# A decoder layer's token mixer issued in the order of a written table, with the compressed branch made for four heads at once

## The chip, the cores and the metric

The kernel runs on one core of a Trainium2 chip. Its time is the time of one execution on the device in microseconds, the median of several runs. In the rows, PE is TensorE (the matrix engine), DVE is VectorE, ACT is ScalarE, POOL is GpSimd and SP is SyncE, which here only issues transfers.

## The reference

One layer on x of 512 rows by 1024 columns in float32: a normed token mixer and a normed SwiGLU, both with a residual.

```python
h = rms_norm(x, attn_pre_norm)
mix = hybrid_mixer(h, ...) # one input projection, two kinds of heads, one output projection
x = x + rms_norm(mix, attn_post_norm)
h = rms_norm(x, ffn_pre_norm)
f = (silu(h @ w_gate) * (h @ w_up)) @ w_down
x = x + rms_norm(f, ffn_post_norm)
```

The mixer has four differential heads (two causal softmax maps of 512 by 512 each, the second subtracted with a factor, times values of 128 columns, then a norm of the head) and eight sparse heads in two groups of four. A sparse head sums three branches, each weighted by a sigmoid gate: selected blocks (with this length all blocks are chosen), a window, and a compressed branch. The compressed branch has 31 compressed keys and values for the whole group, made from blocks of 32 rows by a small two-layer network:

```python
sc = einsum('bghqd,bgnd->bghqn', qb, kc) * scale
pc = masked_softmax(sc, cmp_end[None, :] <= qpos[:, None])
o_cmp = einsum('bghqn,bgnd->bghqd', pc, vc)
...
return gb[..., 0:1] * o_cmp + gb[..., 1:2] * o_slc + gb[..., 2:3] * o_win
```

## The kernel before, in words

Rows are handled in four tiles of 128 (index i). Every factor of a large product is split into a high and a low part in a reduced float32 (names ending in h and l, or whi and wlo for weights, ws for output weights), and a product is three products: high times high, low times high, high times low. A weight is loaded as wraw by SP, ScalarE makes whi and VectorE the difference wlo; wraw, whi and wlo have three buffers each, so a load waits until the load three before it has been split.

The opening loads x as columns (xraw), scales it (xh by ScalarE at L213, xl by VectorE at L222), squares and adds it, and TensorE sums the squares over the columns (ssum), from which VectorE makes the rows' factors rstd; rb is rstd spread over all partitions by TensorE, and the rotary tables are multiplied with it. The products with the input weights (fm, and dv for values) don't wait for rstd; what is made of them does.

A softmax map: scores (sc) by TensorE, the masked scores and the maximum in one instruction by VectorE (L510, tile p, maximum nm), the exponential by ScalarE with the sum in l, the division of rows by l (POOL and ScalarE in sparse heads, POOL and VectorE in differential ones), transposes by TensorE (tr), a high copy by ScalarE (pth, L525) and a low one by VectorE (ptl, L526), and the product with the values (av, avn). A sparse head's result lies in half of opair, and each second head is split into oh and ol. A differential head ends with a norm (ms, rr, rs, rsb, sq) ahead of its oh and ol.

In the compressed branch each sparse head has a score bank scc of which it uses 128 columns (four row tiles times 32), nmc (maximum), pc, l, and pcs: the high and low parts, each twice, so that four 128-column transposes (trc, pct) give a left factor of 128 partitions for the product with vcs, whose four blocks of partitions hold the compressed values high and low.

The products with the output weights are made in two parts: mixp (four of the eight blocks of heads, D0, D1 and the first two sparse pairs) are made during the later heads and copied to SBUF (rope), mix (the other four) for the first two row tiles are made at the end. The norm behind (first instruction mixt) adds both. F0 and F1 are the splits of the first two blocks of feed-forward weights; gain and x are the loads that the norm reads (u is mixt times gain). Behind them come the feed-forward products gu, gw and acc.

Step functions are called in the order of a string:

```python
ORDER = (
    "C v1 q1 q0 k1 cv n1 W0 k0 n0 ck s v0 g W4 D0 D1 W1 N0 N1 N2 N3 W5 N4 W2 W3 N5 D2 M0 N6 W6 W7 M1 M2 M3 D3 F0 F1 N7"
)
...
    def nsa_head(*a):
        with tc.high_priority(offset=HP):
            nsa_head_(*a)
```

Each step writes all its instructions at once; a list scheduler with estimated times then chooses for each engine which ready instruction comes next, with the heads preferred. So the string sets priorities, and not the order on an engine. Tile pools add waits: PSUM has two banks of mm (projections and mix), three of sc, two of tr and one of av, and there are 36 slots of 128 by 512 for split data.

## Time and profile before

| | |
|---|---|
| median of three runs | 669.98 us (669.73 to 670.91) |
| profiled execution | 670.32 us, its span 668.5 us |
| granted TensorE clock, mean | 0.986 |
| TensorE busy | 640.7 us, 96% |
| VectorE busy | 559.3 us, 84% |
| ScalarE busy | 388.6 us, 58% |
| GpSimd busy | 76.4 us, 11% |

A row of a group reads: line, engine, operation, out<-in by the program's names, partitions by elements, xcount, then busy us, mean ns of one, and the idle time of its engine ahead with what ended it. A row of the timeline starts with its start in us and its length. A row of waits gives engine, tile and line, what it waited for, the total in us, how often, and the longest. A row of the stretches gives from:to, length, busy us of each engine (with the number of instructions), the granted TensorE clock, the share of the transfer engines and GB/s.

### The profile page before, as it was taken

The page shows a single profiled execution, that of the slowest core. Times are in us where ns is not written, and L with a number is a line of the kernel's source. Part 1 is how long each engine was busy: PE and PEld are TensorE (multiplying, and loading weights), DVE is VectorE, ACT ScalarE, POOL GpSimd, SP SyncE. Part 2 cuts the span into 40 slices and gives each one's busy share as a digit, 9 for nine tenths or more (in the row PEclk, how much of TensorE's full clock was granted, in tenths as well). Part 3 has the DMA queues.
Part 4 walks back from the last instruction along what each step waited for, and adds up shares of the span by engine and source line. Part 5 has one row for each costly group of instructions (what it writes and reads, how often), then busy time and mean ns, then how long its engine had stood idle before and what let it go on. Part 6 is the DMA issues. An engine that isn't in the chain of part 4 may idle for free.

```text
span 668.5 us, 11185 instructions
## 1 busy us (share of the span) xinstructions
PE 640.7 (96%) x4099; PEld 573.1 (86%) x4099; DVE 559.3 (84%) x1114; ACT 388.6 (58%) x820; POOL 76.4 (11%) x86
## 2 busy tenths in 40 slices
PE   8999999999899998888899999999999999999995
PEld 5988788899778787777898999999999998888884
DVE  4878797897999987768999998888888639999966
ACT  6443453657799766635646555555555547665424
POOL 0000000020755532501100000000000000000023
PEclk9999999999999999979989999999999999999998
DMA  8445767771030530136213323323223217562443
GB/s 307 163 142 204 270 223 280 273 284 56 17 127 18 173 104 24 64 106 241 96 64 126 126 97 114 108 96 122 99 95 127 96 49 251 189 219 96 172 112 126
DMA packets 29735, 94.50 MB, mean 141 GB/s; under 512 B 3824, under 2 KB 4720, under 8 KB 28784
## 3 DMA queue, kind: packets, MB, share of 16 engines
q1 hardware_dynamic: 29104, 92.74, 39.5%
q0 software_dynamic: 576, 1.05, 0.9%
q8 instruction: 32, 0.52, 0.3%
q14 instruction: 23, 0.19, 0.1%
HBM read 80.66 MB, written 12.06 MB: 139 GB/s over the span
## 4 chain that ended last, share of the span: by engine, by line
PE 48%; DVE 3%; ACT 1%; issue 1%; DVEq 0%; ACTq 0%
PE gw L874 28%; PE acc L1166 17%; PE gu L854 4%; DVE mixt L958 1%; DVE rr L958 1%; DVE x L958 1%; DVE htl L958 0%; ACT junkb L958 0%; ACT rr L958 0%; ACT hth L958 0%; DVE ug L1073 0%; ACT L859 0%; DVE ffl L1073 0%; DVE cy L930 0%; DVE u L958 0%
## 5 line engine op out<-in xcount | busy, mean ns | idle before, releaser
L530 POOL TENSOR_TENSOR p<-p,l 128x384 f32<-128x384 f32 (+3 forms) x60 | 49.2, 848 | 130.3 <-DVE l L560 57.3
L116 ACT ACTIVATE whi<-wraw 128x1024 fp32r<-128x1024 f32 (+2 forms) x36 | 37.0, 1038 | 44.1 <-PE fm L302 16.0
L511 ACT ACTIVATE p<-p,nm 128x128 f32<-128x128 f32 (+1 forms) x96 | 53.2, 556 | 15.5 <-DVE nm L510 14.9
L126 DVE TENSOR_TENSOR wlo<-wraw,whi 128x1024 fp32r<-128x1024 f32 (+2 forms) x36 | 42.9, 1197 | 18.8 <-ACT whi L116 18.8
L510 DVE CUSTOM_DVE_ANT_0 p<-sc,mask_b 128x128 f32<-128x128 f32 (+1 forms) x96 | 43.9, 483 | 6.5 <-PE sc L506 5.8
L526 DVE TENSOR_TENSOR ptl<-tr,pth 128x384 fp32r<-128x384 f32 (+1 forms) x60 | 35.7, 596 | 5.9 <-ACT pth L525 5.2
L525 ACT ACTIVATE pth<-tr 128x384 fp32r<-128x384 f32 (+1 forms) x60 | 30.9, 517 | 15.4 <-PE tr L521 14.9
L1248 POOL DMA_DIRECT2D rope<-dp x4 | 3.7, 1127 | 315.8 <-DVE rope L1243 315.8
L521 PE MATMUL tr<-ident,p 128*128 128x128 f32 x200 | 34.4, 290 | 3.7 <-DVE rr L139 2.2
L505 PE MATMUL sc<-kst,qst 128*128 128x128 f32 (+2 forms) x96 | 33.5, 357 | 3.9 <-DVE nm L510 2.8
L302 PE MATMUL fm<-xh,whi 128*128 128x512 f32 x128 | 33.5, 396 | 1.2 <-ACT whi L116 1.2
L302 PE MATMUL fm<-xh,wlo 128*128 128x512 f32 x128 | 32.6, 390 | 0.0
L521 PEld LDWEIGHTS tr<-ident,p 128*128 128x128 f32 x200 | 25.2, 149 | 8.6 <-DVE ptl L526 2.9
L302 PE MATMUL fm<-xl,whi 128*128 128x512 f32 x128 | 32.3, 389 | 0.0
L506 PE MATMUL sc<-kst,qst 128*128 128x128 f32 (+2 forms) x96 | 31.0, 326 | 0.0
L302 PEld LDWEIGHTS fm<-xh,whi 128*128 128x128 f32 x128 | 23.6, 188 | 7.0 <-ACT whi L116 1.9
L302 PEld LDWEIGHTS fm<-xl,whi 128*128 128x128 f32 x128 | 24.0, 188 | 5.0
L302 PEld LDWEIGHTS fm<-xh,wlo 128*128 128x128 f32 x128 | 23.8, 188 | 4.8
L505 PEld LDWEIGHTS sc<-kst,qst 128*128 128x128 f32 x96 | 18.5, 193 | 7.7 <-DVE nm L510 6.0
L1073 ACT ACTIVATE ah<-ff 128x256 fp32r<-128x256 f32 (+1 forms) x28 | 14.4, 513 | 14.6 <-DVE ff L1073 11.2
L930 DVE TENSOR_TENSOR cy<-gw,cy 128x512 f32<-128x512 f32 x19 | 13.0, 686 | 11.5 <-PE gw L874 11.5
L874 PE MATMUL gw<-rope,whi 128*128 128x256 f32 x160 | 22.0, 280 | 0.0
(353 smaller groups left out, 2030.3 us busy)
## 6 DMA issues: line engine op xcount, KB each, us to landing
wraw<-in_wg SPq DMA_DIRECT2D x22, 512.0 KB, 3.2
dr<-in_wd SPq DMA_DIRECT2D x22, 512.0 KB, 3.2
wu<-in_wu SPq DMA_DIRECT2D x19, 512.0 KB, 3.2
wraw<-in_wf SPq DMA_DIRECT2D x16, 512.0 KB, 4.7
qk<-rope SPq DMA_DIRECT2D x7, 1024.0 KB, 4.9
kst<-qk SPq DMA_DIRECT2D x24, 256.0 KB, 3.6
qst<-qk SPq DMA_DIRECT2D x16, 256.0 KB, 3.1
wraw<-in_wo SPq DMA_DIRECT2D x8, 512.0 KB, 3.2
```

The costliest lines, as they stand in the source:

```text
L116: act.activation(dst, src, AF.Copy)
L126: (lo_eng or dve).tensor_tensor(lo[:, :w], raw[:, :w], f32(hi[:, :w]), OP.subtract)
L302: pe.matmul(pt, w[:, k * P:(k + 1) * P], xx[k], start=(n == 0), stop=(n == 3 * NK - 1))
L505: pe.matmul(sv, lhs, kk[:, 0, :w], start=True, stop=False)
L506: pe.matmul(sv, lhs, kk[:, 1, :w], start=False, stop=True)
L510: dve.tensor_tensor_reduce(pt, sv, mask_b[:, (NT - 1 - i) * P:], -1.0, BIG, OP.add, OP.min, nm)
L511: act.activation(pt, pt, AF.Exp, bias=nm, scale=-1.0, accum_out=l[:, i:i + 1])
L521: pe.transpose(tr[:, n * P:(n + 1) * P], pts[i][:, j * P:(j + 1) * P], ident)
L526: dve.tensor_tensor(ptl[:, sl], trv, f32(pth[:, sl]), OP.subtract)
L530: pool.tensor_tensor(p, p, l.to_broadcast(list(p.shape)), OP.mult)
L874: m = pe.matmul(pt, ww[:, k * P:(k + 1) * P], hx[k], start=(start and n == 0), stop=(n == 11), skip_group_check=True)
L1166: m = pe.matmul(pt, x, y, start=(start and n == 0), stop=(stop and n == 2), skip_group_check=True)
```

## The change

The work from the opening to the mix products is cut into 25 generators, one for each kind of work and not for each head (for example A scores, X maxima, E exponentials, Y divisions, Z transposes, H and L the high and low copies, V values, W output weights with F0 and F1, M the mix products, P the projections' products, e the row factors, G the compressed branch). A table of 1487 letters says whose next step is written. The engines' handles are wrapped for that time, so that each engine issues in exactly this order; the scheduler still orders what comes behind (the norms and the feed-forward part, whose code is unchanged). All instructions of the table carry one line number, that of the wrapper, L221.

The compressed branch works on the four heads of a group at once: one score bank of 512 columns, one mask product instead of four, and one instruction of 512 columns where four of 128 stood, twice in all. Its high and low parts are written once (cs, in slots of the split data), the transposes take 64 columns, and the product with the values has 64 partitions on the left and gives high and low parts for all 128 rows of av. It loads q again for itself (eight loads of 256 KB more). The gates are kept as 1 + exp and multiplied into l ahead of the reciprocal, so that each sparse head has one multiplication and one reciprocal of 8 columns where it had three of each of 4. A sparse head's division now starts when both of its maps are there.

```diff
-ORDER = (
-    "C v1 q1 q0 k1 cv n1 W0 k0 n0 ck s v0 g W4 D0 D1 W1 N0 N1 N2 N3 W5 N4 W2 W3 N5 D2 M0 N6 W6 W7 M1 M2 M3 D3 F0 F1 N7"
+PROJ = "C v1 q1 q0 k1 cv n1 k0 n0 ck s v0 g"
+HEADS = "D0 D1 N0 N1 N2 N3 N4 N5 D2 N6 D3 N7"
+WORDER = "4 0 1 5 2 3 6 7 F0 F1"
+TABLE = (
+    "aababaababbbacaaabbbcccPabbbaScSbccccabcSbPPPbcbcbPaPbaSbPdbcPcccSSPSSeeeRPeeeeePPPPPeRRSRaPRPRRPePRSRPK"
...
+    "WWVOOWWWWWMMWWWOWJJMWMMOJWWMWJM"
 )
...
+    class Written:
+        def __init__(self, eng):
+            self.eng, self.begun = eng, False
+
+        def __getattr__(self, name):
+            def issue(*a, **k):
+                r = getattr(self.eng, name)(*a, **k)
+                for x in r if isinstance(r, tuple) else (r,):
+                    if self.begun:
+                        tc.keep_in_program_order(x)
+                    self.begun = True
+                return r
+            return issue
+    act, dve, pool, pe, sp = (Written(e) for e in (act, dve, pool, pe, sp))
...
-    def cmp_head(h, q, l):
-        g = h // HPG
-        st = ps("sc", "scc")
-        for i in range(NT):
-            o = st[:, i * NPAD:(i + 1) * NPAD]
-            pe.matmul(o, q[:, i * P:(i + 1) * P], kch[:, g], start=(i == 0), stop=False)
-            pe.matmul(o, q[:, i * P:(i + 1) * P], kcl[:, g], start=False, stop=False)
-        pe.matmul(st[:, :P], ident_b, cmask_b, start=False, stop=True)
...
+    def compressed():
+        nh = HPG * NT
+        bc = [P, nh, NPAD]
+        for g in range(GROUPS):
+            for hh in range(HPG):
+                yield f"n{g}"
+                q_ = load_q(nq(g), hh)
+                yield "ck"
+                if not hh:
+                    scc = ps("sc", "scc")
+                for i in range(NT):
+                    o = scc[:, hh * P + i * NPAD:hh * P + (i + 1) * NPAD]
+                    pe.matmul(o, q_[:, i * P:(i + 1) * P], kch[:, g], start=(hh == 0 and i == 0), stop=False)
+                    pe.matmul(o, q_[:, i * P:(i + 1) * P], kcl[:, g], start=False, stop=False)
+            pe.matmul(scc.rearrange("p (h n) -> p h n", h=HPG), ident_b,
+                      cmask_b.unsqueeze(1).to_broadcast([P, HPG, P]), start=False, stop=True)
...
+            dve.tensor_reduce(nm, sv, AX.X, OP.max, negate=True)
...
+            dve.tensor_tensor(cv, sv, nm.unsqueeze(2).to_broadcast(bc), OP.add)
+            yield
+            act.activation(cv, cv, AF.Exp)
+            yield
+            dve.tensor_reduce(l, cv[:, :, :NCMP], AX.X, OP.add)
...
+            dve.tensor_tensor(lv, lv, gv, OP.mult)
+            dve.reciprocal(l, l)
+            dve.tensor_scalar(lv[:, :, 0], lv[:, :, 0], valid, None, OP.mult)
+            yield
+            dve.tensor_tensor(cv, cv, l.unsqueeze(2).to_broadcast(bc), OP.mult)
+            cgs[g] = [sslot("cs").rearrange("p (i s n) -> p i s n", s=2, n=NPAD) for _ in range(2)]
+            for j, cs in enumerate(cgs[g]):
+                src = cv[:, j * 2 * NT:(j + 1) * 2 * NT]
+                yield
+                act.activation(cs[:, :, 0], src, AF.Copy)
+                yield
+                dve.tensor_tensor(cs[:, :, 1], src, f32(cs[:, :, 0]), OP.subtract)
+            obj["cgs", g] = True
...
+                dve.tensor_tensor(l, l, gates[:, :, 3 * h + 1:3 * h + 3].rearrange("p i b -> p b i"), OP.mult)
+                dve.reciprocal(l, l)
...
+    need = {t: next(g) for t, g in streams.items()}
+    for t in TABLE:
+        need[t] = next(streams[t], "end")
+    act, dve, pool, pe, sp = nc.scalar, nc.vector, nc.gpsimd, nc.tensor, nc.sync
```

Three places show what the order makes of it.

The first is TensorE in the opening, at the first value products. Before, ssum stands among the first tile's products of dv and rb ahead of the third tile's (tiles' numbers differ between the versions):

```order
L302 MATMUL fm_293<-xl_185,whi 128x512
L376 MATMUL dv_339<-whi,xh_124 128x256
...
L376 MATMUL dv_339<-wlo,xh_146 128x256
L272 MATMUL ssum<-ones,xraw 128x1
L376 MATMUL dv_339<-whi,xh_159 128x256
...
L376 MATMUL dv_339<-whi,xl_181 128x256
L272 MATMUL ssum<-ones,xraw 128x1 x7
...
L278 MATMUL rb<-ident,rstd 128x128 x4
L376 MATMUL dv_395<-whi,xh_124 128x256
```

Now, with fm_171 and fm_240 the two products of the first pair and v the values' products:

```order
L221 MATMUL fm_171<-xl_203,whi 128x512
L221 MATMUL fm_240<-xh_129,whi 128x512
...
L221 MATMUL fm_240<-xh_158,wlo 128x512
L221 MATMUL ssum<-ones,xraw 128x1 x8
L221 MATMUL fm_240<-xh_177,wlo 128x512
L221 MATMUL fm_240<-xh_179,wlo 128x512
L221 MATMUL fm_240<-xh_181,wlo 128x512
L221 MATMUL fm_240<-xh_191,wlo 128x512
L221 MATMUL rb<-ident,rstd 128x128 x4
L221 MATMUL fm_240<-xl_167,whi 128x512
```

All of ssum has moved from the values into the second product, ahead of its last twelve, and rb four products behind it.

The second is VectorE where the first sparse head's weights are made. Before, with ISA the maximum of scores and l_1739 the first head's sums:

```order
L630 RECIPROCAL l_1739<-l_1739 128x4
L406 TENSOR_SCALAR gates<-gates 128x96
...
L407 RECIPROCAL gates<-gates 128x96
...
L631 TENSOR_TENSOR l_1739<-l_1739,gates 128x4 x2
L409 TENSOR_SCALAR gates<-gates,valid 128x8
L631 TENSOR_TENSOR l_1900<-l_1900,gates 128x4
L631 TENSOR_TENSOR l_1739<-l_1739,gates 128x4
L613 TENSOR_TENSOR pc<-pc,l_1739 128x128
...
L618 TENSOR_TENSOR pcs<-pc,pcs 128x4x64
```

Now, for four heads at once, with nmc here also the sums:

```order
L221 TENSOR_SCALAR gates<-gates 128x96
L221 CAST ws_1827<-wraw 128x512
L221 TENSOR_TENSOR nmc<-nmc,gates 128x16
L221 RECIPROCAL nmc<-nmc 128x16
L221 TENSOR_SCALAR nmc<-nmc,valid 128x4
L221 TENSOR_TENSOR l<-l,gates 128x8
L221 RECIPROCAL l<-l 128x8
L221 TENSOR_TENSOR pc<-pc,nmc 128x512
L221 TENSOR_TENSOR ws_1829<-wraw,ws_1827 128x512
...
L221 TENSOR_TENSOR cs<-pc,cs 128x8x32
```

The narrow instructions stand once for four heads, and the wide ones have four times the columns.

The third is VectorE at the end, from the last ptl to mixt. Before, where ol is the split of the last pair of sparse heads:

```order
L526 TENSOR_TENSOR ptl<-tr,pth 128x384
L661 TENSOR_TENSOR opair<-avn,avt 64x256
L664 TENSOR_TENSOR ol_3538<-opair,oh_3537 128x256
L661 TENSOR_TENSOR opair<-avn,avt 64x256
L664 TENSOR_TENSOR ol_3538<-opair,oh_3537 128x256
L958 TENSOR_TENSOR mixt<-mix_3359,rope 128x512
```

Now (L142 is the split of a later feed-forward weight):

```order
L221 TENSOR_TENSOR ptl<-tr,pth 128x384
L221 TENSOR_TENSOR wlo<-wraw,whi 128x1024
L221 TENSOR_TENSOR opair<-av,avt 64x256
...
L221 TENSOR_TENSOR ws_3458<-wraw,ws_3456 128x512
L221 TENSOR_TENSOR ol_3474<-opair,oh_3473 128x256
L221 CAST ws_3480<-wraw 128x512
...
L142 TENSOR_TENSOR wlo<-wraw,whi 128x1024
L221 TENSOR_TENSOR ws_3483<-wraw,ws_3481 128x512
L221 TENSOR_TENSOR ol_3474<-opair,oh_3473 128x256
L1198 TENSOR_TENSOR mixt<-mix,rope 128x512 x4
```

The splits of F0 and F1 have moved from ahead of the last ptl to behind it.

More of the change, by code (lines that the diff above doesn't have):

```diff
@@ L262, in hybrid_block_kernel @@
+    act, dve, pool, pe, sp = (Written(e) for e in (act, dve, pool, pe, sp))
+    xh, xl = [], []
     zero = T.tile([P, GROUPS], F32, bufs=1, name="zero")
[L263 removed]
     rp = [sslot(n, F32) for n in ("cos", "sin", "ckv", "skv")]
     cos, sin, ckv, skv = rp
[L266 to L272 removed]
@@ L324, in qk_pair @@
[L324 to L336 removed]
+    obj = {}
@@ new lines, in row_factors @@
+    def row_factors():
+        yield ["sums", "ident"]
+        ssum = ps("tr", "ssum")[:, :NT]
+        for i in range(NT):
+            for j in range(2):
+                pe.matmul(ssum[:, i:i + 1], obj["sq", j][:, i * P:(i + 1) * P], ones, start=(j == 0), stop=(j == 1))
+        yield
+        v, y, t = (cpool.tile([P, NT], F32, tag=f"rr{j}h", name="rr", bufs=2) for j in range(3))
+        act.activation(y, ssum, AF.Ln, bias=eps, scale=1.0 / D_MODEL)
+        act.activation(y, y, AF.Exp, scale=-0.5)
+        yield
+        dve.tensor_scalar(v, ssum, 1.0 / D_MODEL, EPS, OP.mult, OP.add)
+        yield
+        dve.tensor_tensor(t, y, y, OP.mult)
+        dve.tensor_tensor(t, t, v, OP.mult)
+        dve.tensor_scalar(t, t, -0.5, 1.5, OP.mult, OP.add)
+        dve.tensor_tensor(rstd, y, t, OP.mult)
+        yield
+        rb = ps("tr", "rb")
+        for i in range(NT):
+            pe.matmul(rb[:, i * P:(i + 1) * P], rstd[:, i:i + 1].to_broadcast([P, P]), ident, start=True, stop=True)
+        yield
+        dve.tensor_scalar_mul(nrstd, rstd, -1.0)
+        for j in (2, 3, 0, 1):
+            yield ("rope", j)
+            dve.tensor_tensor(rp[j], rb, rp[j], OP.mult)
+            obj["table", j] = True
@@ new lines, in hybrid_block_kernel, with transposes @@
+    mats = [(tok, br) for tok in HEADS.split() for br in range(1 if tok[0] == "D" else 2)]
+    def transposes():
+        for mat in mats:
+            for js in GROUPED:
+                yield ("a",) + mat
+                tr, n = ps("tr", "tr"), 0
+                for j in js:
+                    for i in range(j, NT):
+                        pe.transpose(tr[:, n * P:(n + 1) * P], obj[("a",) + mat][i][:, j * P:(j + 1) * P], ident)
+                        n += 1
+                obj["tr", mat, js[0]] = tr[:, :n * P].rearrange("p (j q) -> p j q", q=P)
@@ new lines, in parked @@
+    def parked():
+        for i in range(NT):
+            for c in range(2):
+                yield ("mixp", i, c)
+                if not i and not c:
+                    mixw[:] = [rope_tile() for _ in range(2)]
+                mixp[2 * i + c] = f32(mixw[i // 2][:, 2 * (i % 2) + c])
+                act.activation(mixp[2 * i + c], obj["mixp", i, c], AF.Copy)
+    streams = {"a": x_loads(), "b": x_highs(), "c": x_lows(), "d": constants(), "e": row_factors(), "S": weights(), "P": projections(), "R": evictions(), "K": compression(), "G": compressed(), "T": turned(),
+               "Q": loads(), "A": scores(), "X": maxima(), "E": exponentials(), "Y": scalings(), "Z": transposes(),
+               "H": highs(), "L": lows(), "V": values(), "O": outputs(), "J": heads(), "W": out_weights(),
+               "M": mixes_(), "U": parked()}
```

1114 lines of the change are left out of this document (625 added, 489 removed).

## The prediction

> **What bounds the kernel now.** I read the page first: the span and how full the engines are.
>
> ```profile
> span 668.5 us, 11185 instructions
> PE 640.7 (96%) x4099; PEld 573.1 (86%) x4099; DVE 559.3 (84%) x1114; ACT 388.6 (58%) x820; POOL 76.4 (11%) x86
> ```
>
> The profiled execution took 670.32 us, 1.8 us beside its span; the median of the runs is 669.98 (669.73 to 670.91). All sums below are made against 670.32, and the 0.34 us to the median is less than I can resolve. Two runs of this kernel can't be told apart below about 0.2%, 1.3 us.
>
> TensorE looks like the bound everywhere, but an average hides stages. So next I read the busy time by stretch, with borders where the last work of a head or of the norms begins: heads D0 and D1 end at 164 and 177, N5 at 258.67, the last transposed block of N7 at 299.76, and the first sum of the first norm (mixt) starts at 303.63.
>
> ```profile
> core 0: us, PE busy (x) PEld busy (x) DVE busy (x) ACT busy (x) POOL busy (x), PEclk, DMA share, GB/s
> 0.00:164.39 164.39, 160.31 (x921) 138.45 (x922) 128.12 (x255) 84.38 (x163) 5.54 (x11) 1.00 0.63 223
> ...
> 177.36:258.67 81.31, 78.27 (x489) 66.47 (x487) 73.15 (x231) 66.35 (x187) 35.60 (x40) 1.00 0.28 92
> 258.67:299.76 41.09, 35.02 (x201) 30.42 (x201) 31.15 (x81) 21.76 (x56) 12.37 (x12) 0.88 0.18 60
> 299.76:303.63 3.87, 2.50 (x13) 2.04 (x12) 1.62 (x4) 1.48 (x4) 0.00 (x0) 1.00 0.95 281
> 303.63:335.57 31.94, 28.31 (x183) 24.61 (x181) 28.85 (x69) 20.54 (x59) 5.14 (x4) 1.00 0.40 153
> 335.57:547.50 211.93, 211.93 (x1730) 209.75 (x1731) 177.37 (x252) 116.38 (x203) 0.00 (x0) 0.99 0.30 104
> ```
>
> From 335.57 on TensorE never pauses, and the change leaves that part as it is. The projections up to 164.39 are 97.5% full. What can move is the stretch between, and of it the 122.4 us from 177.36 to 299.76. The norm chain from 303.63 to 335.57 runs one after another, so **the time is decided by when mixt starts and by whether the norm finds its inputs**.
>
> Within the first part of that stretch:
>
> ```profile
> 173.00:232.00 59.00, 54.87 (x359) 46.35 (x358) 56.21 (x186) 49.90 (x146) 32.52 (x37) 1.00 0.27 86
> 232.00:254.00 22.00, 22.00 (x125) 18.88 (x124) 17.88 (x47) 14.12 (x35) 7.43 (x9) 1.00 0.33 109
> ```
>
> Up to 232, VectorE is 95% full and the bound; after it, TensorE. From 254 on nobody is full, and the longest waits of TensorE say why: the maxima (nm) and the norm of a D head (rr).
>
> ```profile
> PE sc L505 <- DVE nm L510: 2.8, 3, 1.8
> PE tr L521 <- DVE rr L139: 2.2, 1, 2.2
> ```
>
> Each such pause costs twice: after a pause of 1.8 us the clock is halved for some 3.4 us.
>
> ```profile
> 261.50:263.33 1.83, 0.05 (x1) 0.00 (x0) 1.64 (x4) 1.17 (x2) 1.83 (x2) 1.00 0.00 0
> 264.50:267.90 3.40, 3.40 (x17) 2.96 (x16) 3.29 (x12) 2.43 (x9) 0.02 (x1) 0.50 0.00 0
> ```
>
> **The compressed branch.** These are VectorE's rows that go, and two that price what comes (a reciprocal of 8 columns, a two-operand instruction of 512):
>
> ```profile
> L631 DVE TENSOR_TENSOR l<-l,gates 128x4 f32<-128x4 f32 x24 | 5.5, 234 | 0.5
> L618 DVE TENSOR_TENSOR pcs<-pc,pcs 128x256 fp32r<-128x256 f32 x8 | 5.4, 670 | 0.0
> L630 DVE RECIPROCAL l<-l 128x4 f32<-128x4 f32 x24 | 4.1, 172 | 1.0 <-ACT p L511 0.7
> L613 DVE TENSOR_TENSOR pc<-pc,l 128x128 f32<-128x128 f32 x8 | 2.9, 357 | 0.1
> L603 DVE TENSOR_REDUCE nmc<-scc 128x4 f32<-128x128 f32 x8 | 2.3, 285 | 0.3
> L606 DVE TENSOR_TENSOR pc<-scc,nmc 128x128 f32<-128x128 f32 x8 | 2.3, 283 | 0.1
> L608 DVE TENSOR_REDUCE l<-pc 128x4 f32<-128x124 f32 x8 | 2.2, 272 | 0.2 <-ACT pc L607 0.2
> L559 DVE RECIPROCAL l<-l 128x8 f32<-128x8 f32 x4 | 0.8, 198 | 0.2 <-ACT p L511 0.2
> L685 DVE TENSOR_TENSOR ws<-wraw,ws 128x512 fp32r<-128x512 f32 x12 | 8.4, 697 | 0.1
> ```
>
> Out: 5.5+5.4+4.1+2.9+2.3+2.3+2.2 = 24.7 us. In: eight products and eight reciprocals of 8 columns (8 x 0.43 = 3.5), per group of four heads four wide instructions (8 x 0.70 = 5.6), three narrow ones (6 x 0.2 = 1.2), and four splits of 256 columns at 0.4 to 0.67 (2.2 in the middle). That is 12.5, so VectorE loses some 12 us, all of it in the stretch of the heads. TensorE's work stays the same within 1 us: the seven products that are gone are small, and the turned blocks are half as high but still 32. ScalarE loses 2 to 3 us. Eight more loads of q (256 KB each) go to SP's queue; the DMA share there is 0.28, so I cost them at nothing; if they came late, the first scores of a group would wait.
>
> **The order in the heads.** Products overlap in the rows, so I price one by the distance to the next:
>
> ```profile
> 19.39 2.65 PE L302 MATMUL fm<-xl,whi 128*128 128x512 f32 x11
> L302 PE MATMUL fm<-xl,whi 128*128 128x512 f32 x128 | 32.3, 389 | 0.0
> ```
>
> Eleven products of 512 columns take 2.65 us, and the last one's own 0.39: (2.65 - 0.39) / 10 = 0.227 from start to start. With such distances I added up each engine's instructions in program order between the same landmarks. From D1's end to N5's end, VectorE goes from 72 to 56 us (9 from the compressed branch, 5.6 because two wlo, two casts and three ws are moved behind, the rest maxima that are issued earlier), and TensorE from 72.3 to 61.8, since 39 of the 88 products mixp leave for the part behind N5 (39 x 0.227 = 8.9). From N5's end to the last ptl, TensorE goes from 30.1 to 34.2, VectorE from 32 to 30. The mixp there are what was missing: ready work for the pauses. An N head's scalings now wait for both its maps; I cost that at nothing, as POOL, which does most of them, was busy for 35.60 of 81.31 us, and the next head's scores lie ready on TensorE; without that cover each head's transposes would come a map later.
>
> So TensorE becomes the bound of the first part: 61.8 us if nothing is lost, 69.5 if it loses the same 81.31/72.3 as before. I take 5% (65 us), since in 232 to 254, where VectorE had air, TensorE was full. The second part lies between 34.2 and 46.8 (the old loss, 41.09/30.1); I take 10%, 37.6.
>
> A rule of the Trainium skill speaks on the pauses: "TensorE: Matmul & The Clock Gate", in its table "Why this matters for your kernels", allows idle gaps of up to about 3 us before the clock falls. This trace does not bear it out: the pause above was 1.8 us long. By the rule the 2.4 us pause that I expect on TensorE in the new tail would cost nothing more; by the trace 1.7 us, half of the 3.4 at 0.50, on products that lie beside VectorE's tail.
>
> **The opening.** Here the change moves the row factors (ssum, rstd, rb) forward, into the second product fm of the first pair.
>
> ```profile
> 11.13 3.41 PE L302 MATMUL fm<-xh,whi 128*128 128x512 f32 x12
> 11.44 2.55 ACT L213 ACTIVATE xh<-xraw,gc 128x512 fp32r<-128x512 f32 x4
> 12.71 4.72 DVE L222 SCALAR_TENSOR_TENSOR xl<-xraw,gc,xh 128x512 fp32r<-128x512 f32 x7
> 22.28 0.73 PE L376 MATMUL dv<-whi,xh 128*128 128x256 f32 x4 [0.23 <-ACT craw L318]
> 24.74 1.62 PE L272 MATMUL ssum<-ones,xraw 128*128 128x1 f32 x14
> 27.71 0.16 DVE L146 TENSOR_TENSOR rstd<-rr 128x4 f32<-128x4 f32 x1
> ```
>
> Before, the two products were interleaved, so that xh and xl came in time, and ssum and rb lay among products of v. Now one runs after the other: the first waits for xh (1.2 us) and xl (0.5). The xl end at 12.71 + 8 x 0.66 = 18.0, and the six sums of squares (0.65 each) and ident at about 22.1, where TensorE arrives at 21.0 (18.3 and 12 products; 1.1 wait, and behind ssum stand the rest of fm and all of v). From ssum to rstd it took 1.5 us, of which four products hide 0.9 (0.6 wait). Together 3.4, less the 0.8 that TensorE stood still before between 11.13 and 22.28 (46 products there, 10.4 us, in 11.15): **+2.6 us**, and TensorE is full up to D1, so it stays.
>
> **The tail.** With T the end of the last ptl:
>
> ```profile
> L118 DVE CAST ws<-wraw 128x512 fp32r<-128x512 f32 x18 | 9.3, 517 | 0.4 <-DMA wraw<-in_wo 0.4
> L126 DVE TENSOR_TENSOR wlo<-wraw,whi 128x1024 fp32r<-128x1024 f32 x33 | 40.1, 1221 | 17.6 <-ACT whi L116 17.6
> 299.20 0.56 DVE L526 TENSOR_TENSOR ptl<-tr,pth 128x384 fp32r<-128x384 f32 x1 [1.55 <-ACT pth L525]
> 303.63 2.49 DVE L958 TENSOR_TENSOR mixt<-mix,rope 128x512 f32<-128x512 f32 x4
> 298.05 0.90 SPq L777 DMA_DIRECT2D gain<-in_grow  x2
> DMA to landing us min/median/max: 4.3/5.5/7.5
> 306.21 1.29 DVE L958 TENSOR_TENSOR u<-mixt,gain 128x512 f32<-128x512 f32 x1
> 304.40 2.55 POOL L986 TENSOR_TENSOR u<-mixt,gain 128x512 f32<-128x512 f32 x2 [23.13 <-DVE mixt L958]
> ```
>
> mixt stood 3.87 us behind T. Now the splits of F0 and F1 stand between: three wlo (3.7), four casts (2.1), four ws (2.8), with opair and ol 1.7 as before: 10.3 us, and some 2.4 of waits (3.87 less 1.7 before). So mixt starts at T + 12.7, and the 24 products mix that TensorE has left (5.4 us) lie beside it. And gain: its load stands on SP behind a load of wg that needs the buffer of the last ws. Before it was issued 5.6 us ahead of mixt (298.05 against 303.63); now right at mixt. It lands 5.5 us later. POOL's u wanted it 0.8 behind mixt (4.7 late), VectorE's u 2.6 behind it (2.9 late), and everything of the norm hangs on u; between the two I take **+4.1 us**, since POOL's is the longer piece.
>
> **The sum.** D1's end 177.36 + 2.6 = 180.0; + 65.0 = 245.0; + 37.6 = 282.6 = T; mixt at 295.3, 8.3 earlier than 303.63; + 4.1 for gain leaves 4.2 us: 670.32 - 4.2 = 666.1.
>
> **The rivals.**
> *The tail costs nothing* (0.25): casts and splits fall into VectorE's waits and gain's load is issued in time; then mixt comes at T + 8 or earlier and the chain keeps its 31.94: 666 - 4.7 - 4.1 = 657. For it: 30 us of VectorE work in 37.6 leaves air ahead of T. Against: the order on VectorE is fixed, with these rows behind the last ptl.
> *The end takes all back* (0.20, slower): the pauses of the D3 and N7 chains stay, the second part keeps its old loss (46.8), T = 291.8, and the tail's 8.8 + 4.1 weighs more than the 8 gained: 670.3 + 5.0 = 675. It decides as soon as T falls by less than 12.9 us, that is T above 286.9. For it: a fixed order can't step round a late instruction; every wait of one engine holds all behind it.
> *The change doesn't do what it says* (0.12, no change): the heads keep the old loss in the first part only (69.5) and all else is as summed, 666.1 + 4.5 = 670.6. TensorE's work is the same, which speaks for it.
> *My forecast*, 661 to 669: 0.43.
>
> **The numbers.** Faster holds my forecast nearly whole and the first rival: 0.66. Same 0.13, slower 0.21. The range goes from 655 (the first rival with 2 us less loss in the heads) to 674, which leaves out the worse half of the second rival.
>
> **What would show it.** Right: the last ptl at 278 to 287; VectorE under 90% between D1 and N5, TensorE over 94%; mixt 11 to 13 us behind the last ptl; gain landing 5 us after mixt starts; dv's first product at 24 to 25.5 plus the factors. Wrong: TensorE's clock at 0.5 several times in the heads (then a pause that the table made), the last ptl behind 287, or gain in time. The prediction fails most easily in the 5% and 10% of loss: each 5% of both is 4.8 us.

## The result and the profile after

The changed kernel takes 679.65 us in the median of eleven runs (676.68 to 685.42); the kernel before, beside it on the same chips, 671.88 (669.68 to 676.66). The ratio is 1.0119, with an interval of 1.0082 to 1.0157: the change made the kernel slower by 1.2%, where 666 was forecast. The profiled execution took 679.65 us. (The table of letters has 1383 of them, not 1487 as the text on the change says.)

The page's first rows, as before:

```profile
span 677.8 us, 11093 instructions
PE 644.9 (95%) x4093; PEld 574.4 (85%) x4093; DVE 552.1 (81%) x1057; ACT 385.4 (57%) x810; POOL 78.0 (12%) x86
```

VectorE is busy 7.2 us less, and the span is 9.3 us longer: the work that went was not what set the end. The stretches, with borders at the same landmarks as before (D1's end, N5's end, the last ptl, mixt), show where it went:

```profile
184.19:253.91 69.72, 66.88 (x431) 57.66 (x430) 56.64 (x176) 58.64 (x166) 34.63 (x39) 0.98 0.32 103
253.91:293.20 39.29, 37.77 (x224) 32.08 (x223) 34.10 (x81) 25.92 (x70) 17.77 (x18) 1.00 0.21 75
293.20:306.49 13.29, 10.65 (x42) 8.33 (x41) 9.13 (x16) 3.63 (x7) 0.00 (x0) 0.87 0.43 158
```

With the first sum of the residual (x, 5.50 us behind mixt before, 10.47 now) and the end of the span, the balance in us is:

| from | to | before | now | change | forecast |
|---|---|---|---|---|---|
| start | D1's end | 177.36 | 184.19 | +6.8 | +2.6 |
| D1's end | N5's end | 81.31 | 69.72 | -11.6 | -16.3 |
| N5's end | last ptl (T) | 41.09 | 39.29 | -1.8 | -3.5 |
| T | mixt | 3.87 | 13.29 | +9.4 | +8.8 |
| mixt | x | 5.50 | 10.47 | +5.0 | +4.1 |
| x | end | 359.4 | 360.9 | +1.5 | 0 |

So the heads did get shorter, by 13.4 us, and the ends on both sides took 21.2 back, with 1.5 more in the code that is unchanged. TensorE's longest waits now are others than before, where the maxima and a head's norm stood:

```profile
PE trh L1260 <- DVE mixt L1198: 7.8, 4, 5.5
PE sc L221 <- DMA kst<-qk: 3.3, 2, 1.8
PE mix L221 <- DVE ol L221: 3.2, 2, 2.6
PE tr L221 <- POOL p L221: 1.5, 2, 0.9
PE ms L221 <- ACT sq L221: 1.5, 1, 1.5
```

trh is the transpose behind the norm, mix the last products of the heads, kst the keys of a map. Each such wait stands in one place of the program, which the timeline gives. First the tail, whose order on VectorE the prediction showed:

```profile
297.88 0.42 DVE L221 TENSOR_TENSOR opair<-av,avt 64x256 f32<-64x256 f32 x1 [3.07 <-ACT avt L221]
302.10 0.42 DVE L221 TENSOR_TENSOR ol<-opair,oh 128x256 fp32r<-128x256 f32 x1
302.57 0.50 PE L221 MATMUL mix<-ws,ol 128*128 128x512 f32 x1 [2.64 <-DVE ol L221]
306.49 2.48 DVE L1198 TENSOR_TENSOR mixt<-mix,rope 128x512 f32<-128x512 f32 x4
306.63 0.91 SPq L1017 DMA_DIRECT2D gain<-in_grow  x2
307.58 2.91 SPq L1026 DMA_DIRECT2D x<-in_x  x4
314.33 0.69 DVE L1198 TENSOR_TENSOR u<-mixt,gain 128x512 f32<-128x512 f32 x1 [5.30 <-DMA gain<-in_grow]
316.96 2.12 DVE L1198 SCALAR_TENSOR_TENSOR x<-u,rr,x 128x512 f32<-128x512 f32 x2 [0.23 <-DMA x<-in_x]
```

VectorE waits 3.07 us for the last values (TensorE makes 15 products mix first), does the splits of F0 and F1 in between, and only then the ol for which TensorE stands still 2.64 us. gain is issued 0.14 us behind mixt's start, and VectorE waits 5.30 us for it. Second the keys of the second group of sparse heads, third the first scores of D0 and the end of D1:

```profile
199.98 2.70 SPq L221 DMA_DIRECT2D qst<-qk  x2
202.74 2.37 SPq L221 DMA_DIRECT2D kst<-qk  x4
207.44 1.84 PE L221 MATMUL sc<-kst,qst 128*128 128x128 f32 x6 [1.44 <-DMA kst<-qk]
```

```profile
116.62 1.04 PE L221 MATMUL sc<-kst,qst 128*128 128x128 f32 x6 [1.81 <-DMA kst<-qk]
177.09 1.05 PE L221 MATMUL ms<-ones,sq 128*128 128x1 f32 x8 [1.49 <-ACT sq L221]
180.13 0.48 PE L221 MATMUL tr<-ident,p 128*128 128x128 f32 x1 [0.85 <-POOL p L221]
```

SP stands 2.7 us at two loads of q, and the four loads of kst, whose buffers are free, stand behind them. What the pauses cost in clock stands in stretches; D1's end is at 184.19, and 173 to 232 and 230 to 280 answer to the 173 to 232 and 232 to 254 of before:

```profile
116.60:126.60 10.00, 9.98 (x55) 8.76 (x56) 7.30 (x22) 5.65 (x14) 0.00 (x0) 1.00 0.76 280
180.00:184.19 4.19, 4.06 (x18) 3.48 (x19) 3.75 (x8) 2.10 (x5) 2.43 (x4) 0.59 0.00 0
184.19:190.00 5.81, 5.51 (x41) 4.50 (x40) 4.90 (x18) 4.77 (x14) 4.66 (x6) 1.00 0.00 0
230.00:280.00 50.00, 50.00 (x304) 43.48 (x303) 42.02 (x124) 40.72 (x116) 19.01 (x23) 1.00 0.26 86
173.00:232.00 59.00, 53.80 (x346) 45.96 (x345) 49.52 (x147) 46.96 (x133) 33.30 (x36) 0.94 0.29 96
200.00:210.00 10.00, 8.26 (x54) 7.42 (x53) 7.77 (x23) 7.91 (x24) 5.98 (x6) 0.87 0.56 185
300.00:310.00 10.00, 7.43 (x26) 5.97 (x27) 8.86 (x18) 4.06 (x11) 0.00 (x0) 0.83 0.58 212
320.00:330.00 10.00, 5.90 (x25) 5.14 (x26) 9.27 (x22) 5.83 (x16) 1.28 (x1) 0.50 0.25 102
```

From 230 to 280 TensorE never stops and never loses clock: there the written order does what it was written for. Up to 232 VectorE has fallen from 95% to 84% (49.52 of 59), but TensorE has not filled up in return, and its clock has fallen to 0.94.

### The profile page after: what moved, and what is told of

It reads as the page before. It is cut to its first block, busy times and chain, and to the rows that moved or that the text cites. A ratio compares the mean times of both kernels' runs of the same rounds, so it can differ in the third digit from the quotient of the medians.

```text
span 677.8 us, 11093 instructions
## 1 busy us (share of the span) xinstructions
PE 644.9 (95%) x4093; PEld 574.4 (85%) x4093; DVE 552.1 (81%) x1057; ACT 385.4 (57%) x810; POOL 78.0 (12%) x86
## 4 chain that ended last, share of the span: by engine, by line
PE 51%; DVE 3%; DMA 2%; ACT 2%; issue 1%; POOL 0%; SPq 0%; DVEq 0%; ACTq 0%
PE gw L1114 28%; PE acc L1406 16%; PE gu L1094 5%; DMA x<-in_x 1%; PE mix L221 1%; DMA wraw<-in_wg 0%; DVE ws L221 0%; PE trh L1260 0%; DVE x L1198 0%; DVE mixt L1198 0%; DVE ol L221 0%; PE av L221 0%; DVE rr L1198 0%; ACT hth L1198 0%; DVE ptl L221 0%
## 5 line engine op out<-in xcount | busy, mean ns | idle before, releaser
L221 POOL TENSOR_TENSOR p<-p,l 128x384 f32<-128x384 f32 (+3 forms) x60 | 51.0, 879 | 136.2 <-DVE l L221 112.0
L221 ACT ACTIVATE p<-p,nm 128x128 f32<-128x128 f32 (+1 forms) x96 | 52.9, 554 | 1.3 <-DVE nm L221 1.3
L221 DVE TENSOR_TENSOR wlo<-wraw,whi 128x1024 fp32r<-128x1024 f32 (+2 forms) x34 | 40.2, 1195 | 12.6 <-ACT whi L221 12.6
L221 DVE CUSTOM_DVE_ANT_0 p<-sc,mask_b 128x128 f32<-128x128 f32 (+1 forms) x96 | 44.3, 482 | 6.8 <-PE sc L221 5.9
L221 ACT ACTIVATE whi<-wraw 128x1024 fp32r<-128x1024 f32 (+2 forms) x34 | 34.8, 1033 | 24.8 <-PE fm L221 14.9
L221 PE MATMUL sc<-kst,qst 128*128 128x128 f32 (+1 forms) x192 | 43.3, 343 | 3.4 <-DMA kst<-qk 3.3
L221 DVE TENSOR_TENSOR ptl<-tr,pth 128x384 fp32r<-128x384 f32 (+1 forms) x60 | 35.1, 597 | 11.1 <-ACT pth L221 10.4
L221 ACT ACTIVATE pth<-tr 128x384 fp32r<-128x384 f32 (+1 forms) x60 | 30.5, 521 | 22.9 <-PE tr L221 22.8
L221 PE MATMUL tr<-ident,p 128*128 128x128 f32 x200 | 31.9, 279 | 2.5 <-POOL p L221 1.5
L221 PE MATMUL fm<-xh,whi 128*128 128x512 f32 x128 | 33.3, 395 | 0.6 <-ACT xh L221 0.2
L221 PEld LDWEIGHTS sc<-kst,qst 128*128 128x128 f32 x192 | 29.1, 197 | 5.5 <-issue 4.0
L221 PE MATMUL fm<-xl,whi 128*128 128x512 f32 x128 | 32.2, 391 | 0.1
L221 PE MATMUL fm<-xh,wlo 128*128 128x512 f32 x128 | 32.2, 391 | 0.0
L221 PEld LDWEIGHTS tr<-ident,p 128*128 128x128 f32 x200 | 24.2, 142 | 8.5 <-POOL p L221 2.2
L221 PEld LDWEIGHTS fm<-xh,whi 128*128 128x128 f32 x128 | 23.7, 188 | 6.7 <-ACT xh L221 2.0
L221 PEld LDWEIGHTS fm<-xl,whi 128*128 128x128 f32 x128 | 23.9, 188 | 5.4 <-DVE xl L221 0.5
L221 PEld LDWEIGHTS fm<-xh,wlo 128*128 128x128 f32 x128 | 23.8, 188 | 4.9
L1313 ACT ACTIVATE ah<-ff 128x256 fp32r<-128x256 f32 (+1 forms) x28 | 14.4, 513 | 14.6 <-DVE ff L1313 11.2
L221 PE MATMUL av<-pth,vn 128*128 128x512 f32 (+1 forms) x64 | 21.8, 346 | 0.6 <-ACT pth L221 0.3
L221 DVE TENSOR_TENSOR rope<-rope 128x512 f32<-128x512 f32 (+1 forms) x30 | 20.8, 711 | 1.8 <-ACT rope L221 1.4
```

Source lines behind the costliest of these rows:

```text
L221: r = getattr(self.eng, name)(*a, **k)
L1313: r = getattr({"a": act, "d": dve}[eng], op)(*a, **k)
```

## The experiments

**My theory** after the two traces: the loss is three places in which something in a fixed order stands behind something that it doesn't need. Loads of gain and x behind weight loads on SP (5 us); the last values and their ol behind mix products on TensorE and behind splits on VectorE (4 us); keys behind loads of q on SP (3 us). **The rivals**: the opening's new order of row factors is what costs; or the fixed order as such does, or the compressed branch of four heads.

Each ratio below is against the kernel before on the same chip, with its interval; the change itself stands at 1.0119. Two numbers of profiled executions should not be subtracted lightly: kernels of one and the same text up to D1 reached D1's end between 183.40 and 189.52. Effects are read from the ratios, mechanisms from lengths within one trace.

**Gain and x first.** The weight loads of the feed-forward part that wait for a buffer are issued behind the loads of gain and x.

```diff
+    def load_w_behind(src):
+        with tc.issue_after(last_x):
+            return load_w(src)
...
-        return [split_w(load_w(w[f])) for w in (wg, wu)]
+        return [split_w(load_w_behind(w[f])) for w in (wg, wu)]
```

> The loads of the third and later feed-forward weights stand behind the loads of gain and x on SP; nothing else changes. Theory (the norm chain waits for gain, which SP issues 0.1 us behind mixt instead of 5.6 us ahead of it, and for x behind it): gain lands before mixt, the first x of the norm comes 5.5 us behind mixt as before (in the changed kernel 10.5), and the time falls by 5 to 6 us, to 1.2 to 2.2 us above the kernel before for a time of about 674. Rival (the norm chain is held by something else, such as TensorE's remaining products mix): gain in time, but under 1.5 us less.

Measured: 674.51 us, ratio 1.0036 (1.0012 to 1.0060), that is 0.83% or 5.6 us less than the change, as expected. Its timeline:

```profile
298.81 0.90 SPq L1021 DMA_DIRECT2D gain<-in_grow  x2
308.93 2.48 DVE L1203 TENSOR_TENSOR mixt<-mix,rope 128x512 f32<-128x512 f32 x4
309.69 2.55 POOL L1231 TENSOR_TENSOR u<-mixt,gain 128x512 f32<-128x512 f32 x2 [13.74 <-DVE mixt L1203]
314.06 1.41 DVE L1203 SCALAR_TENSOR_TENSOR x<-u,rr,x 128x512 f32<-128x512 f32 x2
```

gain is issued 10 us ahead of mixt, GpSimd's u starts 0.8 us behind mixt, and x comes 5.1 us behind mixt instead of 10.47. The place of a few loads on one queue was worth 5.6 us; my forecast had priced 4.1 of them.

**The opening undone.** The row sums come behind the first eight products of v again, in the table alone (P is a projection's product, e a step of the row factors, R an eviction).

```diff
-...SSPSSeeeRPeeeeePPPPPeRRSRaPRPRRPePRSRPK"
+...SSPSSRPPPPeeePPePPeeeeeRRSRaRRRPePRSRPK"
```

> In the table only: ssum stands behind the first eight products of v and rb in the second tile of v, so that no product of fm waits for the sums of squares. Theory (the row factors moved forward cost 3.0 us and TensorE is full behind them): TensorE reaches the middle of the projections 2 to 3 us earlier and the time falls by 2 to 3 us, to about 677. Rival (what is saved at the opening is lost later, at the scores of D0, which wait for their keys until 116.6 us, or in the heads): under 1 us.

Measured: 685.0 us, ratio 1.0199 (1.0173 to 1.0226): slower still, by 0.8%.

```profile
37.30 0.85 DVE L221 SCALAR_TENSOR_TENSOR dv<-v,rstd,dv 128x256 fp32r<-128x256 f32 x2
37.82 1.23 PE L221 MATMUL v<-whi,xh 128*128 128x256 f32 x4 [5.21 <-DVE dv L221]
```

The first v comes at 24.03 instead of 27.98, but v's evictions now stand on VectorE behind ten instructions that make the rotary tables and use them (30.73 to 37.30), and TensorE, whose banks are full, waits 5.21 us. The clock stood at 0.50 from 36 to 42 us besides. A product made early is worth nothing if what empties its bank comes late.

**The tail re-ordered.** In the table's last 40 letters the value products (V) and the ends of the last pair (O, J) go ahead of the mix products (M) and of the splits (W).

```diff
-    ...VVVWMMMMM"
-    "WWVOOWWWWWMMWWWOWJJMWMMOJWWMWJM"
+    ...VVVVWMWWO"
+    "MWOMMWWWJOMJOJJMMMMMMMWWWWWWWWW"
```

> In the table only, from N7's last value products on: these stand ahead of the products mix, both halves of opair, oh and ol ahead of F1's splits, and the second wlo of F0 ahead of ol. Theory (at the end VectorE waits 3.1 us for avt, because 15 products mix stand ahead of the last products av, and TensorE waits 2.6 us for ol, which stands behind F1's splits): mixt starts 3 to 5 us earlier behind the last ptl (13.3 us in the changed kernel); the time falls by 3 to 4 us, less what gain's load, still late, takes back (it may take back all of it). Rival (VectorE's work there is the bound, 10.3 us of it): mixt at most 1 us earlier.

Measured: 674.53 us, ratio 1.0053 (1.0024 to 1.0082), 0.66% or 4.4 us less than the change.

```profile
299.94 0.42 DVE L221 TENSOR_TENSOR opair<-av,avt 64x256 f32<-64x256 f32 x1
307.70 1.28 DVE L1198 TENSOR_TENSOR mixt<-mix,rope 128x512 f32<-128x512 f32 x2
```

opair stands 1.6 us behind the last ptl (298.30 in this trace) instead of 4.7, and mixt 9.4 behind it instead of 13.3. The wait of mix for ol falls from 3.2 to 0.5 us.

**Keys ahead.** The keys of the second group are loaded one head earlier, ahead of a load of q.

```diff
+                    if h == HPG - 1:
+                        for m_ in range(2):
+                            obj["kst", 1, m_] = load_k(obj["s"], 2 * m_ + 1)
```

> The keys of the second group of sparse heads are loaded ahead of N3's q instead of behind N4's, so that they no longer stand on SP behind the compressed branch's loads of q, which wait for a buffer of q. Theory (TensorE's wait of 1.4 us for kst at 206 and the halved clock behind it come from those added loads): no wait for kst at 206, clock 1.00 from 200 to 215, and 3 to 4.5 us less, to about 676. Rival (another engine is as late there): the wait moves to VectorE's maxima, under 1 us less.

Measured: 676.99 us, ratio 1.0074 (1.0045 to 1.0103), 0.45% or 3.0 us less. From D1's end to N5's end it took 66.50 us instead of 69.72: the loads that my prediction had "cost at nothing" were worth 3.2 us in this stretch.

**Four buffers for q** (`BUFS` q 2 to 4) takes the same wait away from its other side.

> The changed kernel with four buffers for q instead of two. Theory (the compressed branch's eight added loads of q wait for a buffer on SP and hold the keys of the second group behind them): no wait for kst at 206, the last ptl 3 to 4 us earlier than 293.2, the time 0.4 to 0.6% under the changed kernel, as with the keys loaded earlier. Rival (it was the place of the keys in SP's order and not the buffers): the wait stays, under 0.15%.

Measured: 677.04 us, ratio 1.0075 (1.0047 to 1.0102), the same 0.44%, and again 66.50 us for the stretch.

```profile
196.51 0.32 SPq L221 DMA_DIRECT2D qst<-qk  x1
196.88 3.62 SPq L221 DMA_DIRECT2D kst<-qk  x4
```

The keys' issue starts at 196.88 instead of 202.74, 6 us earlier, since one load of q stands ahead of it that waits for a buffer, where three did. Two edits that share nothing but this wait give the same gain, and the wait is the cause.

**The three together** (gain first, tail re-ordered, keys ahead).

> Three edits at once: gain and x loaded ahead of the third feed-forward weights, N7's last value products and splits ahead of F1's, and the second group's keys loaded ahead of N3's q. Alone they came out 0.8%, 0.7% and 0.45% under the changed kernel. Theory (three separate waits at three places; the tail's edit alone lost part of its gain to gain's late load): together 13 us or more under the changed kernel, 0.990 to 0.995 of the kernel before, 663 to 667 us. Rival (they shorten the same stretch, or the norm chain finds another late input): 1.000 or more.

Measured: 669.16 us, ratio 0.9974 (0.9953 to 0.9996), 1.45% or 9.7 us below the change, where the three alone add up to 13.0 and the theory had 13 or more. The missing part is mostly an overlap: two of the edits take away partly the same wait. In the trace of the tail alone, the scheduler, which orders the loads behind the table, had put one of the four later weight loads ahead of gain and x, where in the changed kernel all four stood ahead. So gain is issued 5.6 us ahead of mixt (307.70), as it was before the change:

```profile
302.14 0.90 SPq L1017 DMA_DIRECT2D gain<-in_grow  x2
```

From T to x the changed kernel takes 23.8 us, gain first 17.3, the tail alone 17.2, and the three together 15.3. Alone the two edits took off 6.5 and 6.6 us, together 8.5. So they were not separate waits, as the theory had it. What is left in these 15.3 us can be seen in the three together:

```profile
298.85 1.28 DVE L1207 TENSOR_TENSOR mixt<-mix,rope 128x512 f32<-128x512 f32 x2
299.61 2.99 POOL L1235 TENSOR_TENSOR u<-mixt,gain 128x512 f32<-128x512 f32 x2 [9.13 <-DVE mixt L1207]
300.05 1.41 DVE L221 TENSOR_TENSOR ws<-wraw,ws 128x512 fp32r<-128x512 f32 x1
301.38 1.51 DVE L221 CAST ws<-wraw 128x512 fp32r<-128x512 f32 x1
302.81 1.28 DVE L1207 TENSOR_TENSOR mixt<-mix,rope 128x512 f32<-128x512 f32 x2
```

With the splits at the table's end (in the tail alone too), two of F1's instructions stand between the halves of mixt, and beside GpSimd's u they take 1.41 and 1.51 us where the same forms take 0.69 and 0.42 in the median of this trace. So mixt comes 7.5 us behind T, but x 7.8 behind mixt, where with gain first it was 5.1. The Trainium skill, "GPSIMD Engine Reference", section "1. Specifications", says that GpSimd and VectorE share their interfaces to SBUF, with contention for VectorE's instructions that read two SBUF operands or run in a two-port mode. The subtraction above, which reads two operands, agrees with it; whether the cast ran in such a mode no row shows.

**The opening once more**, on top of the three: row sums as in the opening undone, and now the evictions of v's first two tiles ahead of the rotary tables.

```diff
-    ...SSPSSeeeRPeeeeePPPPPeRRSRaPRPRRPePRSRPK"
+    ...SSPSSRPPPPeReePPePPeeRReeeSaPPPRRRRRReS"
...
+        for g_ in "ccvvvvcccccccvvvv":
+            yield
+            next(c_ if g_ == "c" else v_, None)
```

> The three edits and a fourth, in the opening: ssum behind the first eight products of v, rb in its second tile, and on VectorE and ScalarE the evictions of v's first two tiles ahead of the first pair's rotary products. Theory (moving ssum back alone was slower because v's evictions stood behind eight rotary instructions on VectorE, for which TensorE waited 5.2 us; with the evictions ahead, the opening costs no more than before): no wait of v for dv, TensorE 2 to 3 us earlier at 100 us, and 0.3 to 0.45% under the three edits. Rival (the compression of keys, which hangs on the rotary products, comes late in its turn): no gain, with a wait of cmp or sc.

Measured: 672.18 us, ratio 1.0009 (0.9989 to 1.0028), 0.35% above the three. The wait for dv of 5.2 us is gone and the first v comes at 23.86, but other waits appear that the three together didn't have: whi 1.5 us, dv 0.7, and 2.3 on keys instead of 1.2. The opening's cost could be moved, not recovered; whether another order recovers it is open.

**The fixed order taken out.** The changed code without the wrapper, so that the scheduler orders it with its own estimates; the heads have no priority over the rest here, which they had before.

```diff
-                        tc.keep_in_program_order(x)
+                        pass
```

> The changed code without the fixed order: the instructions are still written in the table's order, but the scheduler chooses on each engine, without the preference for heads that the kernel before had. Theory (the fixed order holds engines behind late instructions, and the scheduler steps round them): fewer waits in the opening and at 206 us; gain is still late, so 672 to 680. Rival (the order was good and the new waits come from the code): slower than the changed kernel, above 682.

Measured: 687.83 us, ratio 1.023 (1.0195 to 1.0264): not the theory's 672 to 680, but above 682, as the rival had it.

**The compressed branch alone.** The kernel before, in its scheduler's order, with the branch made for four heads at once.

```diff
-    def cmp_head(h, q, l):
+    def cmp_group(g):
...
-            row_scale(1 + br)
-        c, cv = cmp_head(h, q, l)
-        row_scale(0)
+            row_scale(br)
+        if h % HPG == 0:
+            cmp_group(g)
```

> The kernel before with the compressed branch of four heads at once (as in the change: one score bank, cs, 64-column transposes, eight more loads of q, gates kept as 1 + exp), and the scheduler's order. Theory (VectorE loses about 12 us of work in the stretch where it is 95% full, but the loads of q and the later products fill part of it again): 0.990 to 0.998. Rival (TensorE's work is what counts, and it is the same): 0.998 to 1.002; or slower, if the scores of four heads are made ahead of the first head's maps and hold them.

Measured: 689.49 us, ratio 1.0266 (1.0237 to 1.0296): slower, where the theory had it faster. From D1's end to N5's end, in this kernel and in the one with the order taken out:

```profile
177.12:272.95 95.83, 87.49 (x484) 69.19 (x482) 73.38 (x212) 67.70 (x186) 39.67 (x45) 0.93 0.27 84
190.62:274.63 84.01, 79.09 (x468) 65.79 (x467) 58.29 (x170) 61.19 (x171) 33.79 (x39) 0.97 0.24 76
```

95.83 and 84.01 us, against 81.31 before and 69.72 with the written order. One could think that here too the keys behind q are to blame, so the same kernel ran with **four buffers for q**.

> The kernel before with the compressed branch of four heads at once and four buffers for q. With two buffers it took 2.7% more than the kernel before, and lost 3 us around 190 and 10 us around 230, where a group's branch is made. Theory (the four loads of q of a group went through two buffers that the heads' scores need too): at most 0.5% above the kernel before, or faster. Rival (the scheduler puts the group's branch ahead of the heads' own chain, so that VectorE and TensorE serve four heads before one can go on): still 2% or more.

Measured: 688.95 us, ratio 1.0258 (1.0222 to 1.0295): they are not. So the rival of the fixed order falls as far as it was tried: the same code is 1.1% faster with the order than with the scheduler, which here had no preference for the heads; with that preference it was not run. The rival of the branch does not fall whole: left to the scheduler, it costs 2.7% by itself, and the order pays that back in part. What the old branch would give in a written order was not tried.

**Both ends mended.** The three edits, four buffers for q, and F1's casts on ScalarE with half of its low parts on GpSimd, so that VectorE has less between the last ptl and mixt.

```diff
-                        to_r(HIS, hl[0][c], part)
+                        to_r("a" if tok == "F1" else HIS, hl[0][c], part)
...
-                        (pool if tok in POOL_LO else dve).tensor_tensor(hl[1][c], part, f32(hl[0][c]), OP.subtract)
+                        low = pool if tok in POOL_LO or tok == "F1" and not obj[tok] else dve
+                        low.tensor_tensor(hl[1][c], part, f32(hl[0][c]), OP.subtract)
```

> The three edits together (gain and x first, the tail's order, keys earlier) with four buffers for q, and F1's splits taken off VectorE: its casts on ScalarE and the low halves of its first weight on POOL. Theory (with three edits mixt started at 298.85, 4.8 us earlier than before, and the norm lost it again because F1's casts and differences stood between its sums on VectorE, so that the first x came 7.8 us behind mixt instead of 5.5): mixt 12 us or more earlier than in the changed kernel, x 5.5 us behind it, 0.990 to 0.995 of the kernel before. Rival (the norm chain is held by ScalarE or POOL in VectorE's place, or the gated products find their weights late): 0.997 or more.

Measured: 665.81 us against 673.0, ratio 0.9908 (0.9878 to 0.9937). In its trace mixt stands 8.7 us behind T and x 5.1 behind mixt, so x comes 13.9 us behind T, where it came 15.3 behind in the three together; how much of the step from 0.9974 to 0.9908 is the four buffers, and how much F1, was not taken apart. The 12 us by which mixt was to come earlier than in the changed kernel were missed: it came 2.3 earlier (304.17), since D1 ended at 189.52 in this trace. The profiled execution was the slowest (670.30; the others 664.02 to 669.03), with a wait of 2.9 us for D0's keys and a clock of 0.88 between 120 and 140 us, behind it.

**D0's scores later.** On top of that, D0's first four scores and first maximum come 12 products fm later in the table, to give its keys time.

```diff
-    "...RRRdASAPSSAPdXKPPRPEXQKAK..."
+    "...RRRdSPSSPdKPPRPAAAXEXQKAK..."
```

> The last kernel (0.991 of the kernel before), with D0's first four scores and their first maximum twelve products of fm later in the table, so that TensorE doesn't stand still until D0's keys land. Theory (the wait of 1.2 to 2.9 us for kst at about 115 us is one of two reasons why D1 ends later than forecast; TensorE is full behind it): no wait for kst there, D1's last sum 1.5 to 3 us earlier than in the same kernel without this edit, 0.986 to 0.990 of the kernel before. Rival (D0's maxima or the compression of keys come later in their turn and D1's end is set by them): 0.990 to 0.994.

Measured: 665.91 us against 671.83, ratio 0.9915 (0.9885 to 0.9945). The wait for D0's keys is gone from the trace; the median is that of the kernel without it, and the runs lie within 1.7 us (665.39 to 667.10) where they lay within 6.3. The theory's 0.986 to 0.990 was missed. That the wait made the long runs is likely, but not shown: it was six runs each, on two chips, and only one long run has a trace. The stretches of the last kernel, with borders at D1's end, N5's end, T and mixt:

```profile
182.94:249.69 66.75, 65.53 (x431) 56.44 (x430) 56.78 (x176) 58.35 (x166) 34.62 (x39) 1.00 0.30 95
249.69:288.98 39.29, 37.76 (x224) 32.08 (x223) 34.10 (x81) 25.92 (x70) 17.76 (x18) 1.00 0.13 41
288.98:297.72 8.74, 8.74 (x43) 7.36 (x42) 6.52 (x8) 4.80 (x10) 3.00 (x2) 1.00 0.84 270
```

Against before: +5.6 up to D1's end, -14.6 and -1.8 in the heads, +4.9 in the tail, -0.4 up to x, +1.4 behind: 4.8 us less in the span. These two kernels beat both the kernel before and the change.

## Why the prediction was wrong, by its steps

**What bounds the kernel.** Right: the time was decided by when mixt starts and by whether the norm finds its inputs. In the balance above all of the loss but 1.5 us lies ahead of x.

**"VectorE loses some 12 us".** Right, as it was counted. Added up row by row (count times mean), VectorE's instructions fell from 630.0 to 617.6 us, by 12.4, though the ws of the output weights grew from 697 to 841 ns in the mean, 1.7 us in all. The page's busy time fell by 7.2 only, because it counts a time once in which two neighbours overlap: 70.8 us of the 630 before, 65.5 now. So a row that goes is worth less to the engine than its length, by what it overlapped.

**"TensorE becomes the bound of the first part ... I take 5% (65 us)".** This step failed, by 4.7 us: 69.72. The 61.8 us of work and VectorE's air were right (57 of 70 us, 81%, under the 90% named; TensorE busy 96%, over the 94%), and behind 230 TensorE lost nothing. But the largest piece of the loss isn't a share of the work; it is one wait. 3.2 us are the loads of q (1.44 of pause at 206, and 1.7 from the clock, which was halved for 3.4 us behind it), the term **"I cost them at nothing"**: the transfer engines did have room, as I said, but the queue did not; a load that waits for its buffer holds every load behind it. I named the mechanism ("if they came late, the first scores of a group would wait") for the loads of q, and it came for the keys behind them. The experiments with the keys ahead and with four buffers show it twice. The remaining 1.5 us stay open. They are not the clock: behind D1's end it was 1.00 (184.19 to 190), and with the keys ahead it was 1.00 over the whole stretch, which still took 66.50. The waits of TensorE that the profile lists there add up to 1.3 us of the 4.7 between 66.50 and 61.8; the rest lies inside rows that count as busy. So the 5% was too small even without the loads of q.

**"+2.6 us, and TensorE is full up to D1, so it stays".** The 2.6 was right and the rest wrong. TensorE reached the first product of v 5.70 us later (27.98 against 22.28), and ssum and rb, which now stand ahead of it, take some 2.7 of them at the distances of their products: +3.0 (that the three waits were shorter than I made them, 0.2 and 0.4 us for ssum and rb, and the products between slower, cancelled). But up to D1's end 3.8 us more are lost, of which the trace shows 1.1 at D0's first scores (1.81 for keys against 0.7 before), 0.4 in the waits at D1's end (1.49 and 0.85, where before 1.57 and 0.36 stood), and 1.7 in the clock behind them (0.59 from 180.00 to 184.19, where it was 1.00 before). Some 0.6 us stay open, and no run takes the waits at D1's end away. "TensorE is full" was an average of the kernel before; the order that made it full was the thing that the change replaced. This is the other half of the miss: +6.8 for +2.6.

**"I take 10%, 37.6".** 39.29, 1.7 more. The rival of the same place, that this part "keeps its old loss (46.8)", was wrong.

**"mixt starts at T + 12.7".** 13.29. The rows on VectorE were the right ones to add up, but that the sum came so close is luck: VectorE worked 9.13 us there, where I had 10.3, and stood still 4.2, 3.07 of it for avt, where I had "some 2.4 of waits" (and 3.87 less 1.7 is 2.2). The pause of TensorE that I put at 2.4 was 2.64.

**"+4.1 us" for gain.** 5.0. The order of the queue was read rightly; only the landing took 7.6 us instead of the 5.5 I took from before:

```profile
DMA to landing us min/median/max: 4.3/7.6/8.4
```

Two weight loads of 512 KB were issued in the 1.0 us ahead of it, where before there was one. The experiment with gain and x first shows the term by itself.

**The rule on pauses.** By the Trainium skill's "TensorE: Matmul & The Clock Gate", table "Why this matters for your kernels", pauses up to about 3 us should not lower the clock. The pause of 2.64 us at 299.93 was followed by a clock of 0.83 in 300 to 310, which is 1.7 us of full speed, as forecast by the trace; one of 1.44 us at 206 by 0.87 in 200 to 210. The trace again does not bear the rule out. But my own "Each such pause costs twice" doesn't hold either: behind the pause of 1.81 us at 116.62 the clock stayed at 1.00 (the stretch from 116.60). So what a pause costs depends on more than its length, and on what, no run here shows.

**The rivals.** The slower one, "the end takes all back", gave 675 and came nearest; its point of decision, T above 286.9, held (293.2). Its cause did not: it had the loss in the chains of D3 and N7, and the loss lay ahead of N5. "The tail costs nothing" is refuted by 13.29 and 10.47. That the change doesn't do what it says (the old loss in the first part, 69.5 us) had the length of that part almost to the digit, 69.72, but not its cause: where VectorE was the bound, up to 232, it no longer was. Two of my signs of being wrong were there: the last ptl behind 287, and the clock at 0.50 in the heads, behind the wait for keys.

In one sum: of the 13.5 us between forecast (-4.2) and profile (+9.3), 4.2 are the way up to D1, 4.7 the first part, 1.7 the second, 0.6 the tail, 0.9 gain, and 1.5 the unchanged part, where I had nothing (its clock was 0.50 from 320 to 330; the 1.5 was not taken apart). The range's upper end, 674, came from one rival alone; two terms that miss on the same side, as all six did here, were not in it. And the 0.2% at which I thought two runs can be told apart was too fine: eleven runs of before lie 7 us apart, and eleven runs of each gave an interval of plus and minus 0.37%.

## What to carry to other kernels

When an order is fixed by hand, price each queue that issues transfers as an engine of its own: walk down it, find every load that waits for a buffer, and ask what stands behind it that needs nothing. Don't carry an engine's loss over as a percentage of its work; list the waits, one by one, also in the part that seems full, because that fullness belongs to the old order. And a split that is not needed until later still costs its full time when its row lies between the last value and the norm; it belongs on an engine that is empty there, and on VectorE not beside GpSimd's two-operand work, which doubled the subtraction's time here.

## What the runs showed of the hardware

- VectorE's cast of 512 columns took 1.51 us instead of 0.42, and its subtraction 1.41 instead of 0.69, while GpSimd multiplied two operands (2.99 us for two there, 2.55 in the kernel before).
- A load of 512 KB for gain took 7.6 us to land with two weight loads of that size issued in the 1.0 us ahead of it, and 5.5 and 5.8 us in two traces (the kernel before, gain first) with one such load 0.4 us ahead of it.
- A pause of TensorE of 1.44 us was followed by a halved clock for 3.4 us (0.87 from 200 to 210); one of 1.81 us in the same trace was followed by a clock of 1.00. In 320 to 330, in and behind the 5.5 us for trh, it was 0.50 throughout.
- VectorE's instructions overlap their neighbours in the profile: 630.0 us of them, added up one by one, kept it busy for 559.3 us.
- A wait for one transfer (D0's keys) measured 0.7, 1.81 and 2.9 us in the profiles of three kernels; with the longest, the clock was 0.88 between 120 and 140 us behind it, and that execution was 4.5 us above the median of its kernel.
